# Up projection of a hybrid decoder layer: the halo's low parts move into the first term over 260 columns, and its result tiles into other PSUM banks

## The chip, the cores and the metric

The kernel runs on one core of a Trainium2 chip. The metric is the device time of one execution in microseconds (us), the median over several runs. All operands are float32. Products run on TensorE in the float32r form, which keeps fewer bits, so the kernel splits each operand into a high part (its float32r value) and a low part (what is left), and adds three products: high by high, high by low, low by high.

## The reference

One decoder layer over 1024 positions and 16 meta tokens, with model width 1024 and 2816 feed-forward channels. The change lies in the feed-forward part, whose core is this:

```python
def causal_dwconv(x, w, b):
    taps, c = w.shape
    y = lax.conv_general_dilated(x, w[:, None, :].astype(x.dtype), window_strides=(1,),
                                 padding=[(taps - 1, 0)],
                                 dimension_numbers=('NWC', 'WIO', 'NWC'),
                                 feature_group_count=c)
    return y + b.astype(x.dtype)
...
def hybrid_layer(h, ...):
    z = h @ w_in + b_in
    ...
    h = layer_norm(DEEPNORM_ALPHA * h + mixed @ w_out, ln1_g, ln1_b)
    up = causal_dwconv(h @ ffn_w_up, ffn_dw, ffn_dw_b)
    u, g = jnp.split(up, 2, axis=-1)
    f = (jax.nn.gelu(g, approximate=False) * u) @ ffn_w_down
    return layer_norm(DEEPNORM_ALPHA * h + f, ln2_g, ln2_b)
```

The depthwise convolution has three taps over the positions (FFN_TAPS = 3), so each stretch of positions needs the two positions ahead of it. These two are the halo.

## The kernel before

The layer runs stage by stage on one core: input projection, convolution module and attention, the two projections of the branches, the output projection (tiles ps_w, lines 339 to 343), the up projection (tiles px, py, pz, pw, line 1572), and the down projection (tiles ps_x and ps_z, line 1717).

The up projection computes `h @ ffn_w_up` transposed: channels on the partitions, positions in the columns. It uses a Strassen-Winograd scheme with seven products in place of eight, over the two halves of the model width, of the channels (u and g, 2816 each) and of the positions. It goes over FC = 22 chunks of 128 channels. The seven products of a chunk are called B11, B21, BT2, BT4, BT1, BT3 and B22 after their position operand, and they write the result tiles X, Z, X, V4, Y, X, Y in this order; a second product into a tile adds to the first. ScalarE copies some results out (`copy`, line 1584), and VectorE combines them (`tt`, line 1580) into four blocks c11, c21, c12, c22 (u13 and u2 are helpers), each of 514 columns: 2 halo columns and 512 positions. `conv_ffn` (lines 1497 to 1501) applies the three taps: ScalarE the first (line 1499), VectorE the other two (lines 1500 and 1501). `gelu` and `f_out` (lines 1505 and 1509) finish the chunk and store it to HBM.

The 514 columns of a position block are computed in two halves (`SUB`): half 0 has 258 columns (2 of halo and 256), half 1 has 256. A product of one half is 12 matmuls: four blocks k of 128 inputs times three terms. In the code, `ah` and `al` are the high and low part of the weights, and `bmat(sub, q, hl, k)` is the high (0) or low (1) part of the positions. So a product of a chunk is 24 matmuls, and the stage 22 x 168 = 3696. Each result tile is one of four pairs of PSUM banks, 1024 columns wide; half 0 takes columns 254 to 512 (in the pair's first bank), half 1 columns 512 to 768 (in the second). In the order of their allocation pw lies in banks 0 and 1, px in 2 and 3, pz in 4 and 5, py in 6 and 7.

Chunk 0 is a special case. It runs its seven products on half 1 first, and then on half 0, since the operands of half 0 are not ready at the start. After its third product in half 1, `turn` puts the last eight 128x128 transposes (line 1361) into two of the result tiles; ScalarE moves them out (line 1374), and from them VectorE and ScalarE form the operands of half 0 (`form_t2` to `form_t4`, and `bsplit`, whose high part is a ScalarE copy, line 1264, and whose low part a VectorE subtraction, line 1269).

The weights come by DMA into `wr`. ScalarE casts the high part (line 1393), VectorE subtracts the low one (line 1394), after it has formed the sums of weights (line 1411). The order of instructions on each engine is set at build time by a scheduler that goes by the ranks (`rank(...)`) and by explicit `after` edges. The products of the up projection are chained by `after` in the order of the code. The DMAs named here are issued by the queue of SP.

The down projection has eight one-bank tiles D8, named ps_x or ps_z by the half of its products that they belong to.

Of the kernel before, what the change touches and what calls it, by code (L numbers as in the profile page):

```python
# [23 lines left out]
F = mybir.dt.float32  # L24
# [5 lines left out]
P = 128  # L30
# [30 lines left out]
SUB = [(0, 258), (258, HW)]  # L61

# [50 lines left out]
def tile_hybrid_layer(  # L113
# [1113 lines left out]
    def quadrant(sub, kk, h):  # L1227
# [3 lines left out]
    B_AT = [[(RHC, 40), (RHO, 4096 + 40)] + [(OA, OA_UP + i * KC * BS[0]) for i in range(4)] + [(RX, 56)],  # L1231
            [(OC, OC_UP + i * 2048) for i in range(4)] + [(RHC, 4096 + R_DN), (RHC, 2048 + R_DN), (RHC, 6144 + R_DN)]]
    B11, B21, BT2, BT1, BT3, BT4, B22 = range(7)

    def bsum(sub, q, hl):
        n, s = SUB[sub][1] - SUB[sub][0], BS[sub]
        t, o = B_AT[sub][q]
        return t[:, o + hl * 4 * s:o + (hl + 1) * 4 * s].rearrange("p (k n) -> p k n", k=4)[:, :, :n]

    def bmat(sub, q, hl, k):  # L1240
        return bsum(sub, q, hl)[:, k]
# [18 lines left out]
    def bsplit(sub, q, src, cs=slice(None)):  # L1260
        with rank(RK_SUMS):
            hi, lo = (bsum(sub, q, hl)[:, :, cs] for hl in range(2))
            src = wide(src)[:, :, cs]
            ins = nc.scalar.copy(hi, src)
            if (sub, q) in ((0, BT2), (0, BT4), (0, BT1), (0, BT3)):
                if high:
                    after(ins, high[-1])
                high.append(ins)
            line(nc.vector.tensor_tensor(lo, src, f32(hi), OP.subtract))
# [224 lines left out]
    c11, c21, u2 = (FA[:, 4128 + i * HW:4128 + (i + 1) * HW] for i in range(3))  # L1494
    c12, c22, u13 = (RT[:, i * HW:(i + 1) * HW] for i in range(3))

    def conv_ffn(cc, o):
        t = ftmp()
        nc.scalar.activation(t, cc[:, 2:HW], AF.Identity, bias=ffw(3, o), scale=ffw(2, o))  # L1499
        nc.vector.scalar_tensor_tensor(t, cc[:, 1:HW - 1], ffw(1, o), t, OP.mult, OP.add)  # L1500
        nc.vector.scalar_tensor_tensor(t, cc[:, 0:HW - 2], ffw(0, o), t, OP.mult, OP.add)
        return t
# [47 lines left out]
    for c in range(FC):  # L1550
        V4, X, Z, Y = (pup.tile([P, 1024], F, name=n, tag=n) for n in ("pw", "px", "pz", "py"))
        passes = ((1,), (0,)) if c == 0 else ((0, 1),)
        for subs in passes:
            last = subs == passes[-1]
            w_next = iter(range(7))
            a, b = SUB[subs[0]][0], SUB[subs[-1]][1]

            def at(t):
                return t[:, 254 + a:254 + b]

            def prod(q, bank, first):
                if last:
                    w_ahead(9)
                    ah, al = w_ready.pop(0)
                else:
                    ah, al = w_ready[next(w_next)]
                for sub in subs:
                    o = bank[:, 254 + SUB[sub][0]:254 + SUB[sub][1]]
                    for k in range(4):
                        ks = slice(k * P, (k + 1) * P)  # L1570
                        for j, (x, hl) in enumerate(((ah, 0), (ah, 1), (al, 0))):
                            ins = nc.tensor.matmul(o, x[:, ks], bmat(sub, q, hl, k), start=first and k + j == 0,  # L1572
                                                   stop=k == 3 and j == 2, skip_group_check=not first)
                            if k + j == 0 and last_mm:
                                after(ins, last_mm[-1])
                    last_mm.append(ins)
# [17 lines left out]
            if not last:  # L1594
                turn(5, *last_rows, (V4, Z), last_mm, True)
# [33 lines left out]
    D8 = [pdn.tile([P, 512], F, name="ps_" + "xxzzzzxx"[j], tag=f"d{j}") for j in range(8)]  # L1629
    X, Z = ([D8[j] for j in b] for b in ((0, 1, 6, 7), (4, 5, 2, 3)))  # L1630

# [239 lines left out]
```

## Time and profile before

| | us |
|---|---|
| median of 3 runs (lowest to highest) | 1258.69 (1258.04 to 1259.17) |
| profiled execution | 1258.79 |
| its span, first to last instruction | 1257.0 |
| TensorE busy | 1243.3 (99%) |
| VectorE busy | 1076.1 (86%) |
| ScalarE busy | 597.1 (48%) |

The mean granted TensorE clock was 0.998 of full speed. The span and the busy times come from one profiled execution; what lies around the span is 1.79 us of its 1258.79. The page gives the matmuls of the up projection on line 1572 as groups by tile and operands. Their listed durations (276 to 288 ns) overlap, since matmuls are pipelined; the pace is read from the starts of consecutive blocks instead. A name like `px<-OC,RHO` means that the instruction writes px and reads OC and RHO. The engines are PE (TensorE), PEld (its weight load), DVE (VectorE), ACT (ScalarE), SP (SyncE) and POOL (GpSimd).

### The profile page before, as it was taken

To read this page: it belongs to the slowest core of one execution; us is meant where nothing else is said; L and a number is where in the kernel's file an instruction comes from. 1 tells how busy PE (TensorE), PEld (TensorE's weight loads), DVE (VectorE), ACT (ScalarE), POOL (GpSimd) and SP (SyncE) were. 2 spreads that over 40 slices of the span, in tenths; PEclk is the share of its full clock that TensorE was granted. 3 is DMA by queue.
4 is the path that set the end of the run, shared out by engine and by line. 5 is a ranking of instruction groups with operands and counts; after the bars stand their busy time and mean duration, and the time that the engine had idled before them with its cause. 6 is when DMAs were issued, how large, how long until landed. Compare 5 with 4: busy or idle time off the path is not lost.

```text
span 1257.0 us, 23022 instructions
## 1 busy us (share of the span) xinstructions
PE 1243.3 (99%) x9176; PEld 1178.3 (94%) x9176; DVE 1076.1 (86%) x1855; ACT 597.1 (48%) x1108; POOL 7.4 (1%) x8
## 2 busy tenths in 40 slices
PE   9999999999999999999999999999999999999997
PEld 8999999999999999788899999999999998888886
DVE  8989999999978677548899999998989977896697
ACT  8433264655474233344655555455555544445330
POOL 0000000001000000000000000000000000000000
PEclk9999999999999999999999999999999999999999
DMA  6393633422256554222145545454454566998712
GB/s 260 118 299 102 186 89 104 116 81 85 73 156 187 168 154 110 84 101 85 51 171 199 190 177 205 162 207 149 157 199 160 199 226 251 394 346 334 276 60 84
DMA packets 98685, 212.19 MB, mean 169 GB/s; under 512 B 11395, under 2 KB 38595, under 8 KB 98322
## 3 DMA queue, kind: packets, MB, share of 16 engines
q1 hardware_dynamic: 84414, 199.57, 46.6%
q10 hardware_dynamic: 14164, 11.15, 2.8%
q8 instruction: 72, 1.18, 0.4%
q14 instruction: 35, 0.29, 0.1%
HBM read 150.29 MB, written 62.70 MB: 169 GB/s over the span
## 4 chain that ended last, share of the span: by engine, by line
PE 96%; DVE 2%; ACT 1%; DMA 0%; issue 0%; DVEq 0%; SPq 0%; ACTq 0%
PE px L1572 15%; PE py L1572 10%; PE ps_x L1717 9%; PE ps_z L339 8%; PE ps_z L342 8%; PE ps_z L343 8%; PE ps_z L1717 7%; PE ps_p L1171 7%; PE pz L1572 5%; PE pw L1572 5%; PE ps_w L343 2%; PE ps_w L342 2%; PE ps_w L339 2%; PE ps_z L574 2%; PE ps_t L942 1%; PE ps_s L918 1%
## 5 line engine op out<-in xcount | busy, mean ns | idle before, releaser
L339 PE MATMUL ps_z<-RHO,w 128*128 128x256 f32 (+2 forms) x864 | 243.3, 282 | 0.0
L342 PE MATMUL ps_z<-RHO,w 128*128 128x256 f32 (+2 forms) x864 | 242.5, 281 | 0.0
L343 PE MATMUL ps_z<-RHC,w 128*128 128x256 f32 (+2 forms) x864 | 242.4, 281 | 0.0
L342 PEld LDWEIGHTS ps_z<-RHO,w 128*128 128x128 f32 x864 | 162.5, 188 | 0.5
L343 PEld LDWEIGHTS ps_z<-RHC,w 128*128 128x128 f32 x864 | 162.8, 188 | 0.2
L339 PEld LDWEIGHTS ps_z<-RHO,w 128*128 128x128 f32 x864 | 162.6, 188 | 0.1
L748 DVE SCALAR_TENSOR_TENSOR FA<-cin,cdw,FA 128x1026 f32<-128x1026 f32 x120 | 154.5, 1297 | 0.7
L1394 DVE TENSOR_TENSOR RHO<-wr,RHO 128x512 fp32r<-128x512 f32 x94 | 64.1, 690 | 8.0 <-ACT RHO L1393 7.9
L299 ACT CAST w<-wr 128x1024 fp32r<-128x1024 f32 x37 | 38.8, 1048 | 63.4 <-PE ps_z L343 49.9
L1393 ACT CAST RHO<-wr 128x512 fp32r<-128x512 f32 x94 | 56.9, 620 | 24.6 <-DVE wr L1411 12.4
L1411 DVE TENSOR_TENSOR wr<-wr 128x512 f32<-128x512 f32 x88 | 60.8, 691 | 0.1
L757 ACT ACTIVATE FA<-ps_z,colr 128x258 f32<-128x258 f32 (+1 forms) x64 | 30.1, 472 | 60.1 <-PE ps_z L343 52.5
L302 DVE TENSOR_TENSOR w<-wr,w 128x1024 fp32r<-128x1024 f32 x37 | 45.1, 1218 | 8.1 <-ACT w L299 7.9
L1584 ACT COPY FA<-px 128x514 f32<-128x514 f32 (+2 forms) x23 | 13.2, 573 | 78.7 <-PE px L1572 78.7
L1171 PE MATMUL ps_p<-OC,w 128*128 128x256 f32 (+1 forms) x384 | 48.1, 278 | 0.0
L1171 PE MATMUL ps_p<-OA,w 128*128 128x256 f32 (+1 forms) x384 | 47.8, 278 | 0.0
L1171 PEld LDWEIGHTS ps_p<-OC,w 128*128 128x128 f32 x384 | 46.2, 188 | 0.1
L1171 PEld LDWEIGHTS ps_p<-OA,w 128*128 128x128 f32 x384 | 45.9, 188 | 0.0
L1394 DVE TENSOR_TENSOR w<-wr,w 128x512 fp32r<-128x512 f32 x60 | 40.9, 690 | 5.7 <-ACT w L1393 5.6
L1572 PE MATMUL px<-OA,RHO 128*128 128x258 f32 x324 | 43.2, 282 | 0.0
L1499 ACT ACTIVATE FA<-OB,coll 128x512 f32<-128x512 f32 x44 | 35.9, 815 | 14.9 <-DVE OB L1580 14.9
L1572 PE MATMUL px<-OC,RHO 128*128 128x256 f32 x324 | 41.5, 277 | 0.8 <-DVE OB L1327 0.8
(450 smaller groups left out, 3082.0 us busy)
## 6 DMA issues: line engine op xcount, KB each, us to landing
wr<-in_w_up_dram SPq DMA_DIRECT2D x44, 512.0 KB, 3.6
wr<-in_w_z_dram SPq DMA_DIRECT2D x29, 512.0 KB, 4.1
OB<-in_w_down_dram SPq DMA_DIRECT2D x24, 512.0 KB, 4.8
fd<-FA SPq DMA_DIRECT2D x44, 256.0 KB, 2.0
FA<-sd SPq DMA_DIRECT2D x15, 512.0 KB, 8.9
qt<-qd SPq DMA_DIRECT2D x28, 256.0 KB, 4.3
OB<-td SPq DMA_DIRECT2D x14, 512.0 KB, 8.9
sgd<-FA ACTq DMA_DIRECT2D x48, 128.0 KB, 2.7
```

What stands on the lines that cost most here:

```text
L299: ins = nc.scalar.copy(hi, raw)
L302: return nc.vector.tensor_tensor(lo, raw, f32(hi), OP.subtract)
L339: ins = nc.tensor.matmul(ps, al, bh, start=i == 0, stop=False)
L342: nc.tensor.matmul(ps, ah, bh, start=False, stop=False)
L343: last = nc.tensor.matmul(ps, ah, bl, start=False, stop=i == n - 1)
L748: nc.vector.scalar_tensor_tensor(acc[c], cin[:, j:j + U], wc, acc[c], OP.mult, OP.add)
L1171: nc.tensor.matmul(ps[:, :b - a], x, rhs(k, hl, a, b), start=k + j == 0, stop=k == 3 and j == 2)
L1393: nc.scalar.copy(hi, src)
L1394: ins = nc.vector.tensor_tensor(lo, src, f32(hi), OP.subtract)
L1411: ins = nc.vector.tensor_tensor(*x)
L1572: ins = nc.tensor.matmul(o, x[:, ks], bmat(sub, q, hl, k), start=first and k + j == 0, stop=k == 3 and j == 2, skip_group_check=not first)
L1717: nc.tensor.matmul(banks[i], l[:, ts], r[:, ws], start=first and a and x + k == 0, stop=z and x == len(ops) - 1 and k == 2, skip_group_che ...
```

## The change

**Columns and terms.** In half 0 each block of a position operand's high part now has the halo's two low columns in front of it: 260 columns, [2 low halo | 2 high halo | 256 high]. The low part has 256 columns, without the halo. The 12 matmuls of a half-0 product are reordered by term: four of `ah` by the 260 columns, four of `al` by the 260, and four of `ah` by the 256 low columns, which write to columns 256 to 512 of the tile, the place of the 256 positions alone. The first eight write columns 252 to 512. The result's two additional columns hold what the low halo gives, and must be added to the two halo columns behind them. The low halo times `al` is in that sum too. It is of the size of the low by low term, which the scheme leaves out elsewhere. Half 1 is as it was.

**After the product.** The six blocks c11 to u13 are 516 columns wide (CU), and so are the copies and additions on them. `conv_ffn` begins with two ScalarE activations of 128x1, which add the sums of the low halo to the two halo columns: 4 calls a chunk, 22 chunks, 176 instructions.

**Forming the operands.** `bsplit` subtracts the low part in two operations for half 0: one of 256 columns by block (fewer where the operand is split in two steps), and one of 128x4x2 for the halo.

**Banks.** The result tiles are allocated as pw, py, pz, px: px now lies in banks 6 and 7, py in 2 and 3. The last transposes go to (Y, Z), py and pz, in place of (V4, Z), pw and pz. D8's tiles are regrouped to match: ps_x in banks 0 to 3, ps_z in 4 to 7, where they were 0, 1, 6, 7 and 2 to 5.

The start of the up projection on TensorE, before: the last rows of the output projection, then half 1 of chunk 0 with the transposes (line 1361) in it. OC, RHC and OB hold position operands, RHO and w weights.

```order
L343 MATMUL ps_w<-RW,RHO 128x512
L1572 MATMUL px<-OC,RHO 128x256 x12
L1572 MATMUL pz<-OC,RHO 128x256 x12
L1572 MATMUL px<-OC,RHO 128x256 x12
L1361 MATMUL pw<-coll,OB 128x128 x4
L1361 MATMUL pz<-coll,OB 128x128 x4
L1572 MATMUL pw<-RHC,RHO 128x256 x12
L1572 MATMUL py<-OC,w 128x256 x12
```

The same place of the changed kernel:

```order
L344 MATMUL ps_w<-RW,RHO 128x512
L1594 MATMUL px<-OC,RHO 128x256 x12
L1594 MATMUL pz<-OC,RHO 128x256 x12
L1594 MATMUL px<-OC,RHO 128x256 x12
L1379 MATMUL py<-coll,OB 128x128 x4
L1379 MATMUL pz<-coll,OB 128x128 x4
L1594 MATMUL pw<-RHC,RHO 128x256 x12
L1594 MATMUL py<-OC,w 128x256 x12
```

The order of the products is the same; the first four transposes write py, so that the product behind them, BT4 into pw, shares no tile with them, and BT1 into py, one later, does.

ScalarE in a chunk in the middle of the stage, before, from the copy of one chunk's BT3 product to the next copy of px (the first product of the next chunk); FA and OB hold result blocks and temporaries:

```order
L1584 COPY OB<-px 128x514
L1499 ACTIVATE FA<-OB,coll 128x512
L1499 ACTIVATE FA<-FA,coll 128x512
L1393 CAST RHO<-wr 128x512 x2
L1499 ACTIVATE FA<-OB,coll 128x512
L1393 CAST RHO<-wr 128x512
L1584 COPY OB<-px 128x514
```

The same place of the changed kernel:

```order
L1606 COPY OB<-px 128x516
L1518 ACTIVATE OB<-OB 128x1 x2
L1520 ACTIVATE FA<-OB,coll 128x512
L1518 ACTIVATE FA<-FA 128x1 x2
L1520 ACTIVATE FA<-FA,coll 128x512
L1411 CAST RHO<-wr 128x512 x2
L1518 ACTIVATE OB<-OB 128x1 x2
L1520 ACTIVATE FA<-OB,coll 128x512
L1411 CAST RHO<-wr 128x512
L1606 COPY OB<-px 128x516
```

Each of the convolution's first steps has a pair of 128x1 ahead of it; the copies and casts stand in the same order as before.

The diff:

```diff
@@ -59,6 +59,7 @@
 
 HW = 514
 SUB = [(0, 258), (258, HW)]
+CU = HW + 2
 
 W_LEN = 2304
 
@@ -1228,17 +1229,27 @@
         i = h * KC + kk * 4
         return FA[:, h1_at(sub, i):h1_at(sub, i + 4)]
 
-    B_AT = [[(RHC, 40), (RHO, 4096 + 40)] + [(OA, OA_UP + i * KC * BS[0]) for i in range(4)] + [(RX, 56)],
-            [(OC, OC_UP + i * 2048) for i in range(4)] + [(RHC, 4096 + R_DN), (RHC, 2048 + R_DN), (RHC, 6144 + R_DN)]]
+    HP = 264
+    B_AT = [[(RHC, 16, 0), (RHO, 4096 + 16, 0)] + [(OA, 8 + i * 2080, i % 2) for i in range(4)] + [(RX, 32, 0)],
+            [(OC, OC_UP + i * 2048, 0) for i in range(4)] + [(RHC, x + R_DN, 0) for x in (4096, 2048, 6144)]]
     B11, B21, BT2, BT1, BT3, BT4, B22 = range(7)
 
     def bsum(sub, q, hl):
-        n, s = SUB[sub][1] - SUB[sub][0], BS[sub]
-        t, o = B_AT[sub][q]
-        return t[:, o + hl * 4 * s:o + (hl + 1) * 4 * s].rearrange("p (k n) -> p k n", k=4)[:, :, :n]
-
-    def bmat(sub, q, hl, k):
-        return bsum(sub, q, hl)[:, k]
+        r = row(sub, q, hl)
+        return r[:, :, 2:260] if sub == 0 and not hl else r
+
+    def row(sub, q, hl):
+        t, o, back = B_AT[sub][q]
+        hi = HP if sub == 0 else 256
+        o += (4 * 256 if back and not hl else 4 * hi if hl and not back else 0)
+        n = 256 if hl else hi
+        return t[:, o:o + 4 * n].rearrange("p (k n) -> p k n", k=4)
+
+    def bmat(sub, q, j, k):
+
+        if sub:
+            return row(1, q, j % 2)[:, k]
+        return row(0, q, j % 2)[:, k, 0:(260, 256, 260)[j]]
 
     lined, high = [], []
 
@@ -1259,14 +1270,21 @@
 
     def bsplit(sub, q, src, cs=slice(None)):
         with rank(RK_SUMS):
-            hi, lo = (bsum(sub, q, hl)[:, :, cs] for hl in range(2))
             src = wide(src)[:, :, cs]
+            hi = bsum(sub, q, 0)[:, :, cs]
             ins = nc.scalar.copy(hi, src)
             if (sub, q) in ((0, BT2), (0, BT4), (0, BT1), (0, BT3)):
                 if high:
                     after(ins, high[-1])
                 high.append(ins)
-            line(nc.vector.tensor_tensor(lo, src, f32(hi), OP.subtract))
+            n = src.shape[2]
+            a = cs.start or 0
+            x = 2 if sub == 0 and a == 0 else 0
+            a -= 2 if sub == 0 and a else 0
+            lo = bsum(sub, q, 1)[:, :, a:a + n - x]
+            line(nc.vector.tensor_tensor(lo, src[:, :, x:], f32(hi)[:, :, x:], OP.subtract))
+            if x:
+                line(nc.vector.tensor_tensor(row(0, q, 0)[:, :, 0:2], src[:, :, :2], f32(hi)[:, :, :2], OP.subtract))
 
     def bsub(out, x, y, cs=slice(None)):
         with rank(RK_SUMS):
@@ -1491,11 +1509,14 @@
         ft_next[0] += 1
         return FA[:, i * 512:(i + 1) * 512]
 
-    c11, c21, u2 = (FA[:, 4128 + i * HW:4128 + (i + 1) * HW] for i in range(3))
-    c12, c22, u13 = (RT[:, i * HW:(i + 1) * HW] for i in range(3))
+    c11, c21, u2 = (FA[:, 4128 + i * CU:4128 + (i + 1) * CU] for i in range(3))
+    c12, c22, u13 = (RT[:, i * CU:(i + 1) * CU] for i in range(3))
 
     def conv_ffn(cc, o):
         t = ftmp()
+        for i in range(2):
+            nc.scalar.activation(cc[:, 2 + i:3 + i], cc[:, 2 + i:3 + i], AF.Identity, bias=cc[:, i:i + 1], scale=1.0)
+        cc = cc[:, 2:]
         nc.scalar.activation(t, cc[:, 2:HW], AF.Identity, bias=ffw(3, o), scale=ffw(2, o))
         nc.vector.scalar_tensor_tensor(t, cc[:, 1:HW - 1], ffw(1, o), t, OP.mult, OP.add)
         nc.vector.scalar_tensor_tensor(t, cc[:, 0:HW - 2], ffw(0, o), t, OP.mult, OP.add)
@@ -1548,15 +1569,15 @@
     w_first(7)
     pinned_w[0] = False
     for c in range(FC):
-        V4, X, Z, Y = (pup.tile([P, 1024], F, name=n, tag=n) for n in ("pw", "px", "pz", "py"))
+        V4, Y, Z, X = (pup.tile([P, 1024], F, name=n, tag=n) for n in ("pw", "py", "pz", "px"))
         passes = ((1,), (0,)) if c == 0 else ((0, 1),)
         for subs in passes:
             last = subs == passes[-1]
             w_next = iter(range(7))
-            a, b = SUB[subs[0]][0], SUB[subs[-1]][1]
+            a, b = SUB[subs[0]][0] + (2 if subs[0] else 0), SUB[subs[-1]][1] + 2
 
             def at(t):
-                return t[:, 254 + a:254 + b]
+                return t[:, 252 + a:252 + b]
 
             def prod(q, bank, first):
                 if last:
@@ -1565,14 +1586,15 @@
                 else:
                     ah, al = w_ready[next(w_next)]
                 for sub in subs:
-                    o = bank[:, 254 + SUB[sub][0]:254 + SUB[sub][1]]
-                    for k in range(4):
-                        ks = slice(k * P, (k + 1) * P)
-                        for j, (x, hl) in enumerate(((ah, 0), (ah, 1), (al, 0))):
-                            ins = nc.tensor.matmul(o, x[:, ks], bmat(sub, q, hl, k), start=first and k + j == 0,
-                                                   stop=k == 3 and j == 2, skip_group_check=not first)
-                            if k + j == 0 and last_mm:
-                                after(ins, last_mm[-1])
+                    terms = [(k, j) for k in range(4) for j in range(3)]
+                    if sub == 0:
+                        terms = [(k, j) for j in (0, 2, 1) for k in range(4)]
+                    for i, (k, j) in enumerate(terms):
+                        o = bank[:, 512:768] if sub else bank[:, (252, 256, 252)[j]:512]
+                        ins = nc.tensor.matmul(o, (ah, ah, al)[j][:, k * P:(k + 1) * P], bmat(sub, q, j, k),
+                                               start=first and i == 0, stop=i == 11, skip_group_check=not first)
+                        if i == 0 and last_mm:
+                            after(ins, last_mm[-1])
                     last_mm.append(ins)
 
             def tt(*x):
@@ -1592,7 +1614,7 @@
             prod(BT2, X, False)
             copy(u2[:, a:b], at(X))
             if not last:
-                turn(5, *last_rows, (V4, Z), last_mm, True)
+                turn(5, *last_rows, (Y, Z), last_mm, True)
                 for q in (B11, B21):
                     split_of(0, q, LATE)
                 form_t2(0, LATE)
@@ -1626,8 +1648,8 @@
     oa_stack.close()
     dn = ctx.enter_context(tc.tile_pool(name="dn", bufs=1, side="left", reuse_waits="tile"))
     pdn = ctx.enter_context(tc.tile_pool(name="pdn", bufs=1, space=PSUM, reuse_waits="tile"))
-    D8 = [pdn.tile([P, 512], F, name="ps_" + "xxzzzzxx"[j], tag=f"d{j}") for j in range(8)]
-    X, Z = ([D8[j] for j in b] for b in ((0, 1, 6, 7), (4, 5, 2, 3)))
+    D8 = [pdn.tile([P, 512], F, name="ps_" + "xxxxzzzz"[j], tag=f"d{j}") for j in range(8)]
+    X, Z = ([D8[j] for j in b] for b in ((0, 1, 2, 3), (4, 5, 6, 7)))
 
 
     def blk(t, first, step, col):
```

## The prediction

> **What bounds the kernel now.** I read the page first, its busy times and the shares of the chain that ended last.
>
> ```profile
> span 1257.0 us, 23022 instructions
> PE 1243.3 (99%) x9176; PEld 1178.3 (94%) x9176; DVE 1076.1 (86%) x1855; ACT 597.1 (48%) x1108; POOL 7.4 (1%) x8
> ...
> PE 96%; DVE 2%; ACT 1%; DMA 0%; issue 0%; DVEq 0%; SPq 0%; ACTq 0%
> ```
>
> TensorE is the bound nearly everywhere, so a saving counts only if it shortens TensorE's own work or one of its few waits. PEld has one weight load per matmul (9176 of each), so the order of the terms saves and costs no load. Next I asked for TensorE's waits between 570 and 1060 us, which takes in the whole up projection. The columns are total, times and longest, in us.
>
> ```profile
> PE pw L1572 <- ACT FA L1374: 1.2, 1, 1.2
> PE px L1572 <- DVE OB L1327: 0.8, 1, 0.8
> ```
>
> Both waits lie at the start of the up projection. The chain of waits shows where (start, length, engine, tile, line, count).
>
> ```profile
> 602.17 0.70 DVE OB L1327
> 602.92 1.63 PE px L1572 x12
> 604.55 1.36 PE pz L1572 x12
> 605.91 1.36 PE px L1572 x12
> 607.27 0.45 PE pw L1361 x4
> 607.75 1.51 ACT FA L1374 x4
> ...
> 614.90 0.28 ACT OB L1584
> 615.23 1.70 PE px L1572 x12
> 616.93 1.45 PE pz L1572 x12
> 618.38 1.68 PE px L1572 x12
> 620.05 1.44 PE pw L1572 x12
> 621.49 1.45 PE py L1572 x12
> 622.94 1.43 PE px L1572 x12
> ...
> 625.83 2.85 PE px L1572 x24
> ...
> 1039.43 29.94 PE ps_z L1717 x132
> ```
>
> Chunk 0 runs its 256-column half first (602.92 to 615) and then its 258-column half (615.23 to 625.83). From 625.83 on each of the other 21 chunks runs seven products of 24 matmuls, with no wait of TensorE until 1039.43, where the down projection starts. That stretch gives the pace: (1039.43 - 625.83) / 147 products = 2.814 us. A block of twelve 256-column matmuls takes 1.36 us (604.55, 605.91), 113.4 ns each. The twelve of 258 columns then take 2.814 - 1.36 = 1.454 us, 121.1 ns each, and the blocks at 621.49 and 622.94 (1.45, 1.43) say the same.
>
> **The columns: the main term.** Two columns cost 7.7 ns, far more than their share. The next question is what 260 cost. The nearest rows are wider matmuls elsewhere: the 78 matmuls of 384 columns (chain of waits), and 24 of 272 columns, from the first to the start of the 256-column work behind them (timeline of TensorE).
>
> ```profile
> 40.63 13.52 PE ps_z L574 x78
> ```
>
> ```profile
> 53.82 0.34 PE L574 MATMUL ps_z<-RHC,w 128*128 128x384 f32 x1
> 53.99 0.29 PE L339 MATMUL ps_z<-RHO,w 128*128 128x272 f32 x1
> ...
> 57.02 0.28 PE L339 MATMUL ps_z<-RHO,w 128*128 128x256 f32 x1
> ```
>
> 384 columns take 13.52 / 78 = 173.3 ns, 272 take 3.03 / 24 = 126.2, and the 512 of the down projection 29.94 / 132 = 226.8. From 384 to 512 a column costs 0.418 ns, from 258 to 384 it costs 0.414, from 258 to 272 0.36. Carried down to 256 that line gives 120.3 ns, while 113.4 is measured. So a matmul pays about 7 ns once it is wider than 256, and then 0.4 ns a column. By that, 260 columns cost 121.1 + 2 x 0.4 = 121.9 ns.
>
> The change turns the twelve 258-column matmuls of a product's first half into eight of 260 and four of 256. Before: 12 x 121.1 = 1453 ns. After: 8 x 121.9 + 4 x 113.4 = 1429 ns. That is 24 ns less a product, for 22 chunks x 7 = 154 products: **-3.8 us**, all on the path, since nothing else bounds these stretches. The bounds: if 260 cost no more than 258, the gain is 4 x 7.7 = 31 ns, -4.7 us. If 260 already cost what 272 do, 8 x 126.2 + 4 x 113.4 = 1463 ns, 10 more than before: +1.5 us. I take 121.9, since 260 lies two columns from 258 and twelve from 272.
>
> The Trainium skill (TensorE: Matmul & The Clock Gate, section Back-to-back issue gap) gives the isolated gap of a warm matmul as N/2.4 + 2.5 ns, which is linear in the columns with no step at 256. By it the product would go from 12 x 110.0 = 1320 to 8 x 110.8 + 4 x 109.2 = 1323 ns, a loss of 3 ns, +0.5 us in all. This trace does not agree: 113.4 at 256 against 121.1 at 258.
>
> **The start of the up projection.** Two waits change. The first product's px lies in banks 2 and 3, and waits 0.8 us for the evacuation of the last ps_w by VectorE (602.17). After, px lies in banks 6 and 7, which were emptied before, so TensorE goes on at once, some 0.8 us earlier. The transposes at 607.27 went to pw, and the BT4 product to pw waited 1.2 us for ScalarE to empty them. After, they go to py, and BT4 writes pw at once. But the second wait was also cover: behind it ScalarE works without a gap from 607.75 to the copy at 614.90 for which the second half waits at 615.23. That chain starts when the transposes end, so it moves up by the 0.8 us and no more; what TensorE saves at BT4 it waits again ahead of the second half. So I take **-0.8 us**, between 0 (VectorE or ScalarE is held by something else) and -2.0 (both waits vanish). It is nearest to the first, since the copy at 614.90 ends that stretch.
>
> VectorE has seven more operations of 128x4x2, five of them there. The nearest row by size, and the narrowest lead, that of the BT3 operand (its subtraction, and the product that reads it):
>
> ```profile
> L936 DVE TENSOR_TENSOR sm<-sm 128x4 f32<-128x4 f32 x16 | 2.5, 155 | 0.5 <-ACT sm L932 0.5
> ```
>
> ```profile
> 620.98 1.23 DVE L1269 TENSOR_TENSOR OA<-FA,OA 128x1032 fp32r<-128x1032 f32 x1
> ```
>
> ```profile
> 622.78 1.59 PE L1572 MATMUL px<-OA,w 128*128 128x258 f32 x12
> ```
>
> The operand is ready at 622.21, 0.57 us ahead. Four small operations stand before it, at most 4 x 0.155 = 0.62 us and less where they overlap their neighbours; so they cost 0, at worst 0.1 us here and at most 0.3 with the two behind. What hides them is that lead.
>
> **The small additions on ScalarE.** Each call of conv_ffn gets two ACTIVATEs of 128x1, eight a chunk. The nearest row, and the busy times (count) of TensorE, its weight load, VectorE and ScalarE in the steady stretch:
>
> ```profile
> L270 ACT ACTIVATE sd<-mv,eps 128x1 f32<-128x1 f32 (+1 forms) x17 | 4.9, 293 | 44.5 <-DVE mv L265 44.5
> ```
>
> ```profile
> 626.00:1039.00 413.00, 413.00 (x3525) 413.00 (x3524) 376.27 (x601) 218.10 (x358) 0.00 (x0) 1.00 0.51 185
> ```
>
> Eight at 0.293 are 2.3 us a chunk of 19.7, 49 us over 21 chunks: ScalarE rises from 218 to at most 267 of 413 us. It has room, but its order is fixed, and they stand ahead of copies that free a bank. The tightest such place is the copy of the first px product of a chunk (TensorE, then ScalarE, by their timelines):
>
> ```profile
> 704.48 1.61 PE L1572 MATMUL px<-RHC,w 128*128 128x258 f32 x12
> ...
> 710.11 1.60 PE L1572 MATMUL px<-OA,RHO 128*128 128x258 f32 x12
> ```
>
> ```profile
> 707.20 0.81 ACT L1499 ACTIVATE FA<-OB,coll 128x512 f32<-128x512 f32 x1
> 707.92 0.57 ACT L1584 COPY OB<-px 128x514 f32<-128x514 f32 x1
> ```
>
> The copy ends at 708.49 and px is written again at 710.11, 1.6 us later. A pair ahead of L1499 adds 0.6 us at most, which leaves 1.0. VectorE, 376 of 413 us busy, waits mostly for ScalarE's copy of BT3, and hardly for conv_ffn's first step:
>
> ```profile
> DVE OB L1580 <- ACT OB L1584: 23.5, 18, 5.2
> ...
> DVE FA L1500 <- ACT FA L1499: 0.6, 2, 0.3
> ```
>
> So the pairs cost 0 on the path. Their cover is the 1.0 us at px and some 37 us of idle VectorE over the stretch; without it they would cost up to 2.3 us a chunk. The two added columns of the copies and additions (516 for 514) are 0.4% of operations that lie off the path: 0.
>
> **The down projection.** Its tiles keep their products and get other banks; TensorE enters it without a wait now, and the order of the copies ahead of it stays: 0. Its thinnest supply is its sixth pair of blocks, which the last chunk writes out and loads again (VectorE, the queue of SP, VectorE, TensorE):
>
> ```profile
> 1057.53 0.69 DVE L1509 TENSOR_TENSOR FA<-FA 128x512 f32<-128x512 f32 x1
> ```
>
> ```profile
> 1060.26 0.32 SPq L124 DMA_DIRECT2D raw<-fd  x1
> ```
>
> ```profile
> 1065.54 0.69 DVE L1667 TENSOR_TENSOR RHC<-wr,RHC 128x512 fp32r<-128x512 f32 x1 [1.07 <-ACT RHC L1666]
> ```
>
> ```profile
> 1061.05 8.32 PE L1717 MATMUL ps_z<-RHC,RHO 128*128 128x512 f32 x36
> ```
>
> The last twelve of these 36 matmuls start near 1061.05 + 24 x 0.2268 = 1066.5, the operand is ready at 1066.23: a lead of 0.3 us. VectorE's work ahead of 1057.53 starts from the same last products, so it moves up with TensorE and the lead stays: 0 by my reckoning. My upper bound is +1 us: TensorE comes 4.6 us sooner, and a chain of store, load and cast that keeps 1.3 of these 4.6 us uses up the 0.3 and costs 1.0.
>
> **The sum.** 1258.79 us (the profiled execution, 1.79 outside its span) - 3.8 - 0.8 = 1254.2 us. The median of the runs before is 1258.69, 0.1 lower, so I leave it there.
>
> **The rivals.**
> - *260 columns are dear.* They cost what 272 do (+1.5 us, above), or the 7 ns don't come from the width, so that the four low matmuls, which add to a bank that the wider ones began, pay them too: 8 x 121.9 + 4 x 121.1 = 1460 ns, 7 more than before, +1.0 us. With the start's -0.8 it ends at 1259.0 to 1259.5, no change. For it: the trace has no matmul of 260 columns. Against it: 258, 272, 384 and 512 lie on one line, in several parts of the code. Chance 0.07.
> - *No step at all*: only columns count, and the difference of the two halves has another cause (where their rows or outputs lie). A product's first half goes from 12 x 258 = 3096 to 8 x 260 + 4 x 256 = 3104 columns, 8 x 0.418 = 3 ns more, +0.5 us, 1258.5 with the start. For it: the two halves do differ in where they lie. Against it: the 120.3 ns that the line gives at 256, which no 256-column block shows. Chance 0.03. The skill's linear gap, named above, is this case.
> - *ScalarE's pairs delay px (slower).* If the copy of the first px product comes over 1.6 us later than now, TensorE waits in every chunk. It needs three late pairs or a pair that stands behind a wait for VectorE; at 0.4 us past that point it is 21 x 0.4 = 8.4 us, 1262.6. For it: VectorE is 91% busy and conv_ffn's input comes from it. Against it: 1.0 us is left, and the copies stand where they stood. Chance 0.11.
> - *Part of the gain is lost at an edge*: the start moves nothing (+0.8), or the sixth pair of the down projection comes late (+1), so 1255.0 to 1256.0. For it: the 0.3 us lead and ScalarE's closed chain. Chance 0.18.
> - *As forecast*, 1253.0 to 1255.0: chance 0.61.
>
> **The numbers.** 0.2%, 2.5 us, is about what a measurement of this kernel tells from no change; faster means below 1256.2. The forecast and the edge case lie there but for 0.04 of the latter: 0.75. The dear columns and that 0.04, less 0.01 that end past 1261.2, are 0.13 for the same; the pairs and that 0.01 are 0.12 for slower. The range goes from 1252.6 (260 as 258, -4.7, with -1.5 at the start) to 1258.3, which leaves out the pairs and most of the dear columns, some 0.2.
>
> **What would show it.** In the chain of waits of the changed kernel, products of 24 matmuls should take 2.79 us in place of 2.81, and 147 of them 410.0 us in place of 413.6. The first px product should follow ps_w without a wait, BT4 in pw too, and a wait of about 1.3 us for ScalarE's copy of px should stand ahead of the second half. ScalarE should gain 176 instructions of 0.2 to 0.3 us, and TensorE have no wait between 626 and 1036. Products of 2.81 or more would speak for dear columns, a wait of px on L1606 in each chunk for the second rival, a wait in the first pieces of the down projection for the third.

## The result

The changed kernel takes 1254.89 us (median of 6 runs, 1252.71 to 1256.38) against 1258.93 of the kernel before (6 runs, 1258.04 to 1260.84). The ratio is 0.9963, 95% interval 0.9952 to 0.9973: 4.7 us less by the ratio (3.4 to 6.0), where 4.5 were forecast. The page of the changed kernel:

```profile
span 1254.6 us, 23194 instructions
PE 1239.4 (99%) x9176; PEld 1174.1 (94%) x9176; DVE 1078.2 (86%) x1862; ACT 627.2 (50%) x1284; POOL 7.4 (1%) x8
```

This profiled execution took 1256.38 us, the longest of the six. It had lost 3.2 us before its 58th us, ahead of anything that the change touches: the last matmul of 384 columns starts at 57.05, in the kernel before at 53.82.

```profile
57.05 0.34 PE L575 MATMUL ps_z<-RHC,w 128*128 128x384 f32 x1
```

So the two traces are compared stretch by stretch. TensorE's waits between 570 and 1070 us (total, times, longest):

```profile
PE py L1594 <- ACT OB L1606: 1.1, 1, 1.1
PE px L1594 <- ACT OB L1606: 0.4, 1, 0.4
PE ps_z L1739 <- DVE RHC L1689: 0.2, 1, 0.2
```

The two waits of before are gone, two others stand in chunk 0, one in each of its halves, and there is a small new one in the down projection. The chain of waits, from the output projection's end to the steady stretch, and a product near its end:

```profile
604.78 1.41 PE px L1594 x12
606.19 1.41 PE pz L1594 x12
607.60 1.42 PE px L1594 x12
...
614.90 0.55 ACT OB L1606 x2
...
620.12 1.68 PE px L1594 x12
...
627.49 2.79 PE px L1594 x24
...
1025.45 2.77 PE pw L1594 x24
```

A product of 24 matmuls now takes 2.77 or 2.79 us. From the first of chunk 1 to the first matmul of the down projection (1036.40 in the timeline, below) it is 409.08 us for 147 products, 2.783 each, against 413.60 and 2.814: 4.5 us less. From the start of the output projection's last matmul to chunk 1 it is 22.94 us (604.39 to 627.33 in the timeline) against 23.91 (601.75 to 625.66), 1.0 less. From there to the end, the down projection takes 218.18 us against 217.70, 0.5 more.

The stretch from 626 to 1036 us (busy times of TensorE, its loads, VectorE, ScalarE), and half of the small additions (the other 88 read 285 ns):

```profile
626.00:1036.00 410.00, 410.00 (x3538) 410.00 (x3537) 379.80 (x604) 249.73 (x532) 0.00 (x0) 1.00 0.51 186
```

```profile
L1518 ACT ACTIVATE OB<-OB 128x1 f32<-128x1 f32 x88 | 21.0, 286 | 12.6 <-DVE OB L1602 12.6
```

ScalarE is busier by 32 us there, VectorE nearly as before (379.80 against 376.27), and TensorE never waits.

### The profile page after: what moved, and what is told of

Same layout as the page of the kernel before. It is cut to its first block, busy times and chain, and to the rows that moved or that the text cites. A ratio compares the mean times of both kernels' runs of the same rounds, so it can differ in the third digit from the quotient of the medians.

```text
span 1254.6 us, 23194 instructions
## 1 busy us (share of the span) xinstructions
PE 1239.4 (99%) x9176; PEld 1174.1 (94%) x9176; DVE 1078.2 (86%) x1862; ACT 627.2 (50%) x1284; POOL 7.4 (1%) x8
## 4 chain that ended last, share of the span: by engine, by line
PE 93%; DVE 3%; ACT 1%; DMA 1%; issue 1%; SPq 0%; DVEq 0%; ACTq 0%
PE px L1594 14%; PE py L1594 9%; PE ps_x L1739 9%; PE ps_z L340 8%; PE ps_z L343 8%; PE ps_z L344 8%; PE ps_p L1172 7%; PE ps_z L1739 5%; PE pz L1594 5%; PE pw L1594 5%; PE ps_w L344 2%; PE ps_w L343 2%; PE ps_w L340 2%; PE ps_z L575 2%; PE ps_t L943 1%
## 5 line engine op out<-in xcount | busy, mean ns | idle before, releaser
L1606 ACT COPY FA<-px 128x516 f32<-128x516 f32 (+2 forms) x23 | 13.1, 570 | 68.5 <-PE px L1594 68.5
L1594 PE MATMUL px<-OA,RHO 128*128 128x260 f32 x324 | 43.0, 281 | 0.4 <-ACT OB L1606 0.4
L1411 ACT CAST w<-wr 128x512 fp32r<-128x512 f32 x60 | 36.3, 618 | 9.8 <-DMA wr<-in_w_up_dram 5.7
```

Source lines behind the costliest of these rows:

```text
L1594: ins = nc.tensor.matmul(o, (ah, ah, al)[j][:, k * P:(k + 1) * P], bmat(sub, q, j, k), start=first and i == 0, stop=i == 11, skip_group_ch ...
```

## The experiments

All of them in one table. The time is the median beside that of the kernel before on the same chip. "Product" is the mean of the 147 from chunk 1 to the down projection, "half 0" and "half 1" are the means of its two blocks of 12 matmuls, from the starts of the matmuls in the trace; TensorE's waits in `small_x4` are in them. Where there was one run alone, its time tells little: the runs of the kernel before spread from 1258.25 to 1261.90. The readings go by the product there.

| kernel | us (runs) | before | product ns | half 0 | half 1 |
|---|---|---|---|---|---|
| before | | | 2813.6 | 1445 | 1368 |
| changed | 1254.89 (6) | 1258.93 | 2782.9 | 1423 | 1360 |
| banks_only | 1258.60 (11) | 1259.27 | 2813.6 | 1445 | 1368 |
| columns_only | 1254.74 (5) | 1259.27 | 2782.9 | 1423 | 1360 |
| order_only | 1260.14 (10) | 1259.27 | 2823.2 | 1440 | 1383 |
| low_first | 1252.98 (5) | 1259.27 | 2775.2 | 1415 | 1360 |
| no_small | 1254.66 (5) | 1259.14 | 2782.9 | 1423 | 1360 |
| w256 | 1261.61 (1) | 1259.14 | 2838.1 | 1425 | 1413 |
| w258 | 1257.07 (1) | 1259.14 | 2809.5 | 1427 | 1383 |
| w264 | 1255.88 (1) | 1259.14 | 2802.5 | 1442 | 1360 |
| w256_same_start | 1256.37 (1) | 1259.71 | 2792.4 | 1417 | 1375 |
| w260_spaced_256 | 1260.52 (1) | 1259.71 | 2830.2 | 1443 | 1387 |
| small_x4 | 1261.74 (1) | 1259.71 | 2841.3 | 1430 | 1412 |

### The banks alone, the columns alone

`banks_only` is the kernel before with this edit:

```diff
-        V4, X, Z, Y = (pup.tile(...) for n in ("pw", "px", "pz", "py"))
+        V4, Y, Z, X = (pup.tile(...) for n in ("pw", "py", "pz", "px"))
...
-                turn(5, *last_rows, (V4, Z), last_mm, True)
+                turn(5, *last_rows, (Y, Z), last_mm, True)
...
-    X, Z = ([D8[j] for j in b] for b in ((0, 1, 6, 7), (4, 5, 2, 3)))
+    X, Z = ([D8[j] for j in b] for b in ((0, 1, 2, 3), (4, 5, 6, 7)))
```

> The kernel before with one part of the change alone: the result tiles' banks, the transposes into py and pz, the regrouped tiles of the down projection. My theory: the first px product starts without its 0.8 us wait, the wait for the transposes goes, and what BT4 saves is waited again ahead of half 0 for ScalarE's copy of px; products of 24 matmuls stay at 2.81 us. So 0.8 us faster, 1257.9 to 1258.1. Rival: the closed chain on ScalarE does not move, 0.0 us. Second rival: both waits vanish, 2.0 us faster.

It measured 0.7 us less (1258.60 against 1259.27), which by itself is no difference (ratio 0.9995, interval 0.9986 to 1.0004). The trace tells it apart. The waits of before are gone, and these have come:

```profile
PE py L1572 <- ACT OB L1584: 1.0, 1, 1.0
PE px L1572 <- ACT OB L1584: 0.5, 1, 0.5
```

From the output projection's last matmul to chunk 1 it takes 23.13 us against 23.91, 0.8 less; the products are as before. So the two old waits, 2.0 us, gave way to 1.5 us of new ones, both for copies on ScalarE. The other 0.3 us is in no listed wait. Part of it is that the first wait cost more than its listed time: from the last start of ps_w to the first of pz it was 2.64 us before, and is 1.64 now, 1.0 less for a listed wait of 0.8.

`columns_only` is the changed kernel with these lines put back.

> The changed kernel with the banks, transposes and down tiles of before: only the 260 columns, the order of the terms and the small additions. My theory: products of 24 matmuls take 2.78 us as in the changed kernel, the two waits of 0.8 and 1.2 us at the start are back, 3.8 to 4.5 us faster than before. Rival: half of the changed kernel's gain came from the banks in the steady stretch too, then the products stay above 2.80 us and the gain is under 2.5 us.

4.5 us less (ratio 0.9967, interval 0.9954 to 0.9979), products of 2.783 us, and the two old waits are back:

```profile
PE pw L1594 <- ACT FA L1392: 1.2, 1, 1.2
PE px L1594 <- DVE OB L1345: 0.8, 1, 0.8
```

The two parts act apart, and the whole steady gain is that of the second one: columns, order of the terms and place of the rows together.

### The order of the terms

`order_only` is the kernel before with the changed kernel's order of terms, at 258 columns throughout:

```diff
-                    for k in range(4):
-                        ks = slice(k * P, (k + 1) * P)
-                        for j, (x, hl) in enumerate(((ah, 0), (ah, 1), (al, 0))):
+                    terms = [(k, j) for k in range(4) for j in range(3)]
+                    if sub == 0:
+                        terms = [(k, j) for j in (0, 2, 1) for k in range(4)]
+                    for i, (k, j) in enumerate(terms):
```

> The kernel before with the order of the terms alone: half 0 as four matmuls of ah by high, four of al by high, four of ah by low, all of 258 columns. My theory, in which only the width counts: no change, products of 2.81 us, 0.0 us. Rival: the order itself saves the 7 ns that the block of half 1 lost in the changed kernel (1367 to 1360 ns), 154 x 7 ns = 1.1 us faster, products of 2.806 us.

Neither came. It was slower by 0.9 us (ratio 1.0009, interval 1.0000 to 1.0018), and the trace is clear: 2.823 us a product, 1.4 us more over the 147.

```profile
1020.82 2.83 PE px L1573 x24
```

Half 0 itself got 5 ns shorter and half 1, of which not one instruction was touched, 15 ns longer. The pace of a block depends on the block ahead of it: of the twelve, only the first four are slower, 118.9 ns against 113.4 for the other eight. The kernel before has this too, with 115.3 and 113.4. Its blocks of half 1 take 1.36 us (705.93 to 707.29), but 1.38 (711.54 to 712.92) for the operands BT2 and BT3. There half 0 is shorter by as much, so that all seven products take 2.814 us.

```profile
705.93 1.53 PE L1572 MATMUL px<-OC,w 128*128 128x256 f32 x12
707.29 1.61 PE L1572 MATMUL pz<-RHO,w 128*128 128x258 f32 x12
...
711.54 1.54 PE L1572 MATMUL px<-OC,RHO 128*128 128x256 f32 x12
712.92 1.61 PE L1572 MATMUL pw<-OA,w 128*128 128x258 f32 x12
```

### The place of the rows

In the changed kernel the half-0 block takes 1.43 us for five operands (703.89 - 702.46), and 1.41 for BT4 and BT1 (715.02 - 713.61). A group's row names the width of its first matmul; each of these is 8 of 260 and 4 of 256.

```profile
702.46 1.59 PE L1594 MATMUL py<-RX,w 128*128 128x260 f32 x12
703.89 1.52 PE L1594 MATMUL py<-RHC,w 128*128 128x256 f32 x12
...
713.61 1.58 PE L1594 MATMUL pw<-OA,w 128*128 128x260 f32 x12
715.02 1.52 PE L1594 MATMUL pw<-RHC,w 128*128 128x256 f32 x12
```

In these two the low rows lie ahead of the high ones. `low_first` puts them so in six of the seven:

```diff
-        [P, 8376], R, name="OA")
+        [P, 8424], R, name="OA")
...
-    B_AT = [[(RHC, 16, 0), (RHO, 4096 + 16, 0)] + [(OA, 8 + i * 2080, i % 2) for i in range(4)] + [(RX, 32, 0)],
+    B_AT = [[(RHC, 48, 1), (RHO, 4096 + 48, 1)] + [(OA, 40 + i * 2112, 1) for i in range(3)] + [(OA, 6344, 0), (RX, 0, 1)],
```

> The changed kernel with the low rows ahead of the high ones, and both at byte 32 of a 256-byte line, in six of the seven operands of half 0 (in two of them now: BT4 and BT1). In the changed kernel's trace the half-0 block of these two takes 1413 ns, that of the five others 1427. Theory that the place of the rows makes the 14 ns: six blocks of 1413 and one of 1427, four more than now, 4 x 14 ns x 22 = 1.2 us faster than the changed kernel, 5.2 faster than before. Rival, that the tile, the weights or the place in the chunk make them: 0.0 against the changed kernel.

Six operands now take 2.77 us a product, and BT4 (pw), the one left, 2.79:

```profile
626.39 2.77 PE px L1594 x24
...
634.71 2.79 PE pw L1594 x24
```

The mean falls by 7.7 ns, 1.1 us over 147 products. The time is 1252.98 us, ratio to before 0.9950 (0.9937 to 0.9964): of all kernels run, this is the fastest. Its interval overlaps that of the changed kernel; that it is faster than that one rests on the products in the trace. The place of the rows makes the 14 ns, and not the tile or the weights. By the starts, the 14 ns lie in the last four matmuls, those that read the low rows: in the changed kernel they take 114.2 ns each for BT4 and BT1 and 117.7 for the others, while the first eight take 119.5 or 119.6 for all. With the order of the rows their distance changes too (1056 columns from the first high row to the first low one, 1024 the other way), and no run parts the two.

### The width

Four kernels change the width of the first eight matmuls, to ask whether a step behind 256 columns is what half 0 pays. `w256` and `w258` narrow seven of them from the left (the very first stays, since it clears the bank); here for 256:

```diff
-        return row(0, q, j % 2)[:, k, 0:(260, 256, 260)[j]]
+        return row(0, q, j % 2)[:, k, 0:256] if j == 1 else row(0, q, 0)[:, k, (4 if k + j else 0):260]
...
-                        o = bank[:, 512:768] if sub else bank[:, (252, 256, 252)[j]:512]
+                        o = bank[:, 512:768] if sub else bank[:, (256 if j == 1 else 256 if k + j else 252):512]
```

> The changed kernel with the first eight matmuls of a half-0 product 256 columns wide instead of 260, but for the very first, which stays at 260 and clears the bank; the halo's result and the small additions are left out, so the halo columns are not the reference's. The high rows begin 16 bytes later, all else lies where it did. Theory of a step behind 256 columns: the block falls from 1423 ns (mean of the seven in the changed kernel) to 11 x 113.4 + 121.9 = 1369 ns, products of 24 matmuls 2.73 us in place of 2.783. Rival without a step, 0.42 ns a column: 7 x 4 x 0.42 = 12 ns less, products of 2.77 us.

> As the one of 256 columns, with 258: the first matmul of a half-0 product 260 wide, the next seven 258 (the halo's high parts, without the low ones), the last four 256; the small additions are left out, so the halo columns lack the low part. Step theory with 0.4 ns a column behind it: 7 x 2 x 0.4 = 6 ns less than the changed kernel's 1423, products of 2.777 us. Rival that 260 columns cost a step of their own, as 272 do: 7 x 4 = 28 ns less, products of 2.755 us.

`w264` reads four columns more:

```diff
-        return row(0, q, j % 2)[:, k, 0:(260, 256, 260)[j]]
+        return row(0, q, j % 2)[:, k]
...
-                        o = bank[:, 512:768] if sub else bank[:, (252, 256, 252)[j]:512]
+                        o = bank[:, 512:768] if sub else bank[:, (248, 256, 248)[j]:512]
```

> The changed kernel with the first eight matmuls of a half-0 product 264 columns wide: four more columns in front, read from the same row and written beside what is used, rows beginning at the same byte. Step theory with 0.4 ns a column: 8 x 4 x 0.4 = 13 ns more, products of 2.796 us. Rival that only the number of started groups of columns counts: 0, products of 2.783 us.

The narrower kernels are slower than the changed one, not faster. Half 0 at 256 columns takes 1425 ns, 2 more than at 260, and half 1 behind it 1413, 53 more than in the changed kernel. Every block of `w256` has it (708.62 - 707.19 = 1.43, 710.03 - 708.62 = 1.41):

```profile
707.19 1.59 PE L1592 MATMUL pz<-RHO,w 128*128 128x260 f32 x12
708.62 1.58 PE L1592 MATMUL pz<-OC,w 128*128 128x256 f32 x12
710.03 1.59 PE L1592 MATMUL px<-OA,RHO 128*128 128x260 f32 x12
```

In `w258` half 1 takes 1.41 us behind px, BT2 (711.65 - 710.24), and 1.36 behind pw (714.43 - 713.07):

```profile
710.24 1.58 PE L1592 MATMUL px<-OC,RHO 128*128 128x256 f32 x12
711.65 1.58 PE L1592 MATMUL pw<-OA,w 128*128 128x260 f32 x12
713.07 1.52 PE L1592 MATMUL pw<-RHC,w 128*128 128x256 f32 x12
714.43 1.60 PE L1592 MATMUL py<-OA,RHO 128*128 128x260 f32 x12
```

Half 1 was not touched in either. So a 256-column matmul of half 1 runs at 113.3 ns or at 117.8 here, whole blocks at a time, by what ran ahead of it. 264 columns cost 19 ns a block more than 260, against 13 by 0.4 ns a column and 0 by the rival; from 260 upwards the width does cost.

Both narrower kernels also moved the row's first byte. So two more kept it:

```diff
 w256_same_start
+        return row(0, q, j % 2)[:, k, 0:256 if k + j else 260]
 w260_spaced_256
+        if j == 1:
+            return row(0, q, 1)[:, k]
+        t, o, back = B_AT[0][q]
+        o += (4 * 256 if back else 0) + k * 256
+        return t[:, o:o + 260]
```

> The changed kernel with seven of a half-0 product's first eight matmuls reading only the first 256 of the 260 columns, from the same byte as now (in the run with 256 columns before, they began 16 bytes later, and products rose to 2.838 us). Rows stay 264 columns apart, so they begin at bytes 32, 64, 96, 128 of a 256-byte line or 128 behind these. The values are shifted by four positions, so the output is not the reference's. Width theory: the block falls to 1369 ns and products to 2.73 us. Theory that the distance of the rows, and so the bytes at which they begin, sets the pace: no such fall, products of 2.77 us or more.

> The changed kernel with the first eight matmuls of a half-0 product 260 columns wide as now, but read from rows 256 columns apart, so that all four begin at the same byte of a 256-byte line, as the rows of half 1 do. The values read are not the right ones, so the output is not the reference's. Width theory: nothing changes, products of 2.78 us, a block of 1410 to 1430 ns. Theory of the bytes: the block falls to that of half 1, near 1360 ns, and products to 2.72 us.

With rows 264 columns apart and seven matmuls of 256 columns, a block takes 1417 ns, 6 less than with 260, where the step theory had 54 less. Half 1 behind it rises from 1360 to 1375. Two products of `w256_same_start`, half 0 at 1.42 and 1.41 us, half 1 at 1.36 and 1.41:

```profile
710.04 1.58 PE L1594 MATMUL px<-OA,RHO 128*128 128x260 f32 x12
711.46 1.52 PE L1594 MATMUL px<-OC,RHO 128*128 128x256 f32 x12
712.82 1.56 PE L1594 MATMUL pw<-OA,w 128*128 128x260 f32 x12
714.23 1.58 PE L1594 MATMUL pw<-RHC,w 128*128 128x256 f32 x12
715.64 1.57 PE L1594 MATMUL py<-OA,RHO 128*128 128x260 f32 x12
```

With rows 256 apart, the eight of 260 columns take 121.7 ns each by their starts, against 119.5 in the changed kernel, and the block 1443. Half 1 reads 256 columns at this distance and takes 1360 or 1413 a block, 30 to 83 less. That would fit a step behind 256 columns at this distance, but it is not shown: half 1 has another order of the terms, and the four low matmuls of half 0, which also read 256 columns from rows 256 apart, take 117.4 ns and not 113.4. The theory of the bytes, as I put it, fell as well: rows that all begin at the same byte did not bring 260 columns to the pace of half 1. Two blocks of `w260_spaced_256`, with half 1 behind each (1.41 and 1.36), and half 1 of the first operand again one chunk later:

```profile
704.20 1.61 PE L1598 MATMUL px<-RHC,w 128*128 128x260 f32 x12
705.65 1.58 PE L1598 MATMUL px<-OC,w 128*128 128x256 f32 x12
707.06 1.60 PE L1598 MATMUL pz<-RHO,w 128*128 128x260 f32 x12
708.50 1.52 PE L1598 MATMUL pz<-OC,w 128*128 128x256 f32 x12
709.86 1.61 PE L1598 MATMUL px<-OA,RHO 128*128 128x260 f32 x12
...
725.48 1.52 PE L1598 MATMUL px<-OC,RHO 128*128 128x256 f32 x12
726.84 1.61 PE L1598 MATMUL pz<-RHO 128*128 128x260 f32 x12
```

Here half 1's pace alternates from product to product through the whole stretch, 74 blocks of 1413 ns and 73 of 1360. The same operand has 1.41 us in one chunk (707.06 - 705.65) and 1.36 in the next (726.84 - 725.48), so neither the operand nor its tile decides it; the weights lie elsewhere from chunk to chunk, and what the block ahead leaves behind may count.

What stays open is the mechanism: width, distance, first byte, order and what ran ahead may all have a part, and no run here shows the rule.

### The small additions

`no_small` leaves the loop of two activations out of `conv_ffn`; `small_x4` puts six more behind it.

```diff
+        for i in range(6):
+            nc.scalar.activation(cc[:, i % 2:i % 2 + 1], cc[:, i % 2:i % 2 + 1], AF.Identity, bias=cc[:, 2 + i % 2:3 + i % 2], scale=1.0)
```

> The changed kernel without the 176 small additions on ScalarE (the halo columns then lack the low part's share). My theory: they lie off the path, products of 2.783 us and the same time as the changed kernel, 1254 to 1255 us, ScalarE busy some 30 us less. Rival: they cost part of the gain, then it is faster than the changed kernel by over 1 us, in the steady stretch or at the wait of the down projection.

> The changed kernel with four times as many small activations on ScalarE, 704 in place of 176: the six more in each call write halo columns that nothing reads any more. The run without any of them has shown that the 176 cost nothing. My theory: four times as many are 32 x 0.2 = 6.4 us a chunk of 19.5, ScalarE goes to some 15 of 19.5 us and VectorE still does not wait for long, so products stay at 2.783 us and the time within 1 us of the changed kernel. Rival: the copy of px now comes behind up to three times 0.9 us, TensorE waits in each chunk, over 5 us slower.

Without them: 1254.66 us, the same product to a tenth of a ns, ScalarE at 222 in place of 250 us of the stretch. They cost nothing that the product shows, and take 28 us of ScalarE's time, where I had allowed 49. With four times as many, TensorE does wait for the copies of px, and the stretch is 8.6 us longer (147 x 58.4 ns). The listed waits are 5.8 of it:

```profile
PE px L1596 <- ACT OB L1608: 5.8, 6, 2.3
```

The worst is at the start of the steady stretch, where ScalarE runs without a gap up to the copy, in the chain of waits. It has a table load of 1.28 us (ACT_TABLE_LOAD in the timeline) in it as well:

```profile
630.16 1.28 ACT L1528
...
632.08 0.49 ACT OB L1608
...
632.61 3.05 PE px L1596 x24
```

So the rival's mechanism is real, but waits came six times and not in every chunk, and only with four times the load. My expectation of no cost at four times was wrong.

## Why the prediction was right, and where its reason was not

- **The columns, -3.8 us forecast, -4.5 measured** (147 products at 30.7 ns less; `columns_only` alone gave the same product). Half 0 went from 1445 to 1423 ns, 22 less, where the sum had 24. The other 8 ns are half 1, 1368 to 1360, which the sum left at nothing: I read 1.36 us at the start of the stage and took it for all blocks, though some took 1.38. The -3.8 was for 154 products; for these 147 it is -3.5.
- **The step that failed**: "a matmul pays about 7 ns once it is wider than 256". By it, a product was to change by 8 x 0.8 = +6 ns at the eight matmuls of 260 columns, by 4 x -7.7 = -31 at the four of 256, and by nothing in half 1. By the starts, a half-0 matmul took 120.4 ns before. In the changed kernel the first eight take 119.5 and the last four 116.7, so the change is -7, -15 and -8. The narrow matmuls gave half of what was put on them; the wide ones, which were to cost, and half 1, which was to stay, gave the other half. That -24 and -31 lie so near each other is luck: the errors met.
- **The order of the terms, at 0**: it cost 10 ns a product by itself (`order_only`). From there to `columns_only`, which has the same order, the product falls by 40, 17 of them in half 0 and 23 in half 1. How much of the 40 is the width and how much the new place of the rows is open: in the changed kernel's place 256 columns cost hardly less than 260 (`w256_same_start`, 6 ns a block).
- **The line through 258, 272, 384 and 512 columns** was drawn from rows in other places. The 121.9 ns that it gave for 260 was met only where the rows lie 256 apart (121.7 in `w260_spaced_256`); the 258-column rows that it started from lay 260 apart. So what it showed against 256 may have been place as much as width.
- **The rivals on the columns.** That 260 columns cost what 272 do did not come. That the four low matmuls would not drop to 113.4 ns came in part, 116.7. "No step at all" was nearer to the traces than its 0.03, in that the difference of the two halves has causes beside the width; its time, 1258.5, did not come. Nor is the linear gap of an isolated matmul borne out, which the Trainium skill gives (TensorE: Matmul & The Clock Gate, section Back-to-back issue gap): it had +3 ns a product, and -31 were measured. The 0.13 that the prediction gave to "the same" includes the 0.03 of "no step", which its sentence leaves out.
- **The start, -0.8 forecast**: 1.0 less in the changed kernel, 0.8 in `banks_only`. The closed chain on ScalarE held: its first operation behind the transposes came 6.0 us after the last start of ps_w (607.75 - 601.75), and now comes 5.1 after it (609.49 - 604.39), 0.9 sooner. The 1.3 us wait came in two parts, 1.1 before half 1's last product (py, behind the copy of py, which I had not named) and 0.4 at BT2 of half 0. Ahead of half 0 itself there was none: the copy of px now stands directly behind that of py (614.90, x2), and the wait for py had already taken its place.
- **The small additions at 0**: right, by `no_small`. Their price was put too high, 0.293 against 27.6 / 168 = 0.16 us of added busy time in the run.
- **The down projection at 0**: 0.5 us was lost, part of the edge rival's 1 us, in the place it named: the lead of 0.3 us did not stay. VectorE's last multiplication moved up exactly with TensorE (from 1057.53 to 1054.66, down's start from 1039.27 to 1036.40). But the load behind it took longer, 5.0 us from its issue to the cast that waits for it, against 4.2 before. The rows of before, and then of the changed kernel:

```profile
1060.63 0.42 SPq L124 DMA_DIRECT2D wr<-td  x1
```

```profile
1064.88 0.62 ACT L1666 CAST RHC<-wr 128x512 fp32r<-128x512 f32 x1 [1.14 <-DMA wr<-td]
```

```profile
1054.66 0.68 DVE L1530 TENSOR_TENSOR FA<-FA 128x512 f32<-128x512 f32 x1
```

```profile
1057.74 0.42 SPq L125 DMA_DIRECT2D wr<-td  x1
```

```profile
1062.78 0.62 ACT L1688 CAST RHC<-wr 128x512 fp32r<-128x512 f32 x1 [1.91 <-DMA wr<-td]
```

```profile
1036.40 3.82 PE L1739 MATMUL ps_z<-OC,RHC 128*128 128x512 f32 x16
...
1064.18 2.81 PE L1739 MATMUL ps_z<-RHC,RHO 128*128 128x512 f32 x11 [0.15 <-DVE RHC L1689]
```

In five other kernels matmuls at the same place start late too, and the down projection takes longer than the 217.70 us of before: 218.43 in `no_small`, 218.13 in `low_first`, 217.98 in `banks_only`, 217.92 in `columns_only`, 217.77 in `w256_same_start`; only that of `no_small` is listed as a wait. In `small_x4`, which has the whole change and more, nothing is lost (217.70). So the lead was used up with either part alone and kept with both, and no run here settles what decides it.

## What to carry to other kernels

In a stage that TensorE bounds, price a block by the starts of its own blocks, one kind of neighbour at a time, and not by a line through blocks of other widths in other places: the same 256 columns of half 1 took 113.3 or 117.8 ns here. When columns are cut or added, the place of the rows (first byte, distance, which part lies first) moves with them, and is worth trying by itself; here it gave another 1.1 us, by the products, for no work at all. The operations added to an engine that was half idle cost nothing here; four times as many made the copies behind them late.

## What was not expected of the hardware

The untouched half 1, twelve matmuls of 256 columns, takes 1360 or 1413 ns in most blocks (113.3 and 117.8 each), by what ran before it: in `w256` every block is slow, in `w258` only those behind px, and in `w260_spaced_256` every second one. At the start of the changed kernel three blocks of half 1 ran at 1.41 us; in the kernel before the first of them stood behind a wait, and the two others took 1.36. Moving the row's first byte by 16 while narrowing the matmul from 260 to 256 columns made the product 55 ns longer, and putting the low rows ahead of the high ones made a block of the same twelve matmuls 14 ns shorter.
